# Expert gates of a decoder block: one-hot tables from key numbers in PSUM, one more transpose bank, and another order of gathered rows

## The chip, the cores and the metric

One core of one Trainium2 chip runs the whole kernel. The metric is the device time of one execution in microseconds (us); for the kernel before it is the median of three executions.

## What is computed

One decoder layer on 1024 tokens of width 1024, all in float32. The part that matters here is the second half, a product-key retrieval over 128 x 128 = 16384 single-neuron experts: each token has 8 heads, each head picks 16 experts, so a token has 128 picks, each with a first key number, a second key number and a gate.

```
idx = e1 * N_KEYS + e2
gates = jax.nn.softmax(sc, axis=-1)
u = peer_u[ix]
a = jax.nn.gelu(jnp.einsum('td,thkd->thk', hx, u), approximate=False)
vsel = peer_v[ix]
return jnp.einsum('thk,thkd->td', gx * a, vsel)
```

The first half (adaptive norm, one input projection, sliding-window attention beside a short gated convolution, an output projection) runs ahead of it for each group of tokens.

## The kernel before, in words

The tokens are eight tiles of 128. Three stages do the first half, the query projection (`lin_g0q`, `lin_g1q`, `lin_g2q`) and the choice of experts (`top16`, `pairs_head`): the groups are tiles 0 to 2, 3 to 5, and 6 and 7 (tile names with g0, g1, g2). Then follows a long last stage, `dense_experts`.

Two ways lead through the experts. Tiles 0, 1, 3, 4 and 5 are **dense**: every one of the 16384 experts is computed for them by matmul (line 1107 for u, line 1153 for v), and the gates are a table G of experts by tokens, kept in DRAM (`G_d`). Tiles 2, 6 and 7 are **sparse**: the 128 picks of each token are gathered row by row from `peer_u` and `peer_v` by indirect DMAs that GpSimd issues (line 942); VectorE multiplies each gathered u by h2 and sums it (line 963), and adds each gathered v, weighted, to an accumulator (line 970). Both h2 and the accumulator lie in PSUM.

**Dense gates** (`dense_gates1`, lines 792 to 852) make G for one dense tile. `select` (lines 660 to 718) turns ranks into key numbers, three transposes put picks on partitions and tokens on the free dimension (eT, gT), and then tokens go in groups of four, 32 groups for a tile and 160 for the five tiles. For a group, VectorE compares a table of 0 to 127 (`iota4`, bf16, in SBUF) with the second key numbers (line 808, 128 x 512, float32 out) and with the first ones (line 815, 128 x 512, bf16 out). The first table is multiplied by the gates into `og`, on GpSimd (line 825) for two groups of three and on ScalarE (line 821, four instructions) for the third. Four matmuls (line 837) make 128 x 128 of G each, into one PSUM bank; ScalarE copies it out (line 840), and each eighth group starts a DMA to `G_d` (line 845, issued by ScalarE). The matmuls of a group are written behind the tables of the next one (`pend`). There are three buffers for the line 808 table, two for the line 815 table and three for `og`.

**PSUM** has eight banks. From the second stage on, h2 takes two, the accumulator two, the projections two (`ps_a`) and everything else two (`ps_t`: transposes, attention scores, keys, G).

**Order.** The first three stages are written as generators that are run beside each other at fixed rates: in the second stage the gates of tiles 0 and 1 and the first picks of tile 2, in the third stage the gates of tiles 3, 4 and 5. The order in which each engine then takes these instructions is set by a planner with its own costs. The last stage is written out by hand (`manual_schedule`), with the remaining picks paced beside the matmuls (`Beside.run`). In it VectorE, ScalarE and GpSimd split the weights into high and low parts, weigh and add (lines 1074 to 1160). A generator `sparse_experts` (lines 902 to 981) holds the order of the picks: chunks of eight, the v rows of a chunk behind the u rows of the next one. Behind each chunk of u come one Gelu (line 928, ScalarE) and one gate multiplication (line 930, VectorE). The rows of the next tile's h2 are fetched by SyncE (line 933) and copied to PSUM by ScalarE (line 936) behind the tile's last u. Three row buffers serve the gathers in the first stages, seven in the last.

Of the kernel before, what the change touches and what calls it, by code (L numbers as in the profile page):

```python
# [9 lines left out]
F32 = mybir.dt.float32  # L10
# [5 lines left out]
ALU = mybir.AluOpType  # L16
# [68 lines left out]
def block_kernel(  # L85
# [67 lines left out]
    with ExitStack() as fctx:  # L153
# [36 lines left out]
        for i in range(7):  # L190
            pt = bank("t", f"selT_ps{i}")
            nc.tensor.transpose(pt[:14, :P], sel[:, i, :], ident)
            nc.vector.tensor_copy(selT[:, i, :], pt[:14, :P])
        iota4 = sl_.tile([P, NK, 4], BF16, name="iota4")
        nc.gpsimd.iota(
            iota4, pattern=[[1, NK], [0, 4]], base=0, channel_multiplier=0, allow_small_or_imprecise_dtypes=True
        )
        class Weights:

# [460 lines left out]
        def select(i):  # L660

            sc_ = scv[i]
            if i in SPARSE:
                gt = cst.tile([P, P], F32, tag="gates", name=f"gates{i}", bufs=len(SPARSE))
            else:
                gt = sl_.tile([P, P], F32, tag="gatesd", name=f"gates{i}")
            g3 = gt.rearrange("p (k h) -> p h k", h=8)
            nc.vector.tensor_tensor(g3, sc_, sc_[:, :, 0:1].to_broadcast([P, 8, 16]), op=ALU.subtract)
            nc.scalar.activation(gt, gt, AF.Exp)
            gsu = sl_.tile([P, 8], F32, tag="gs", name=f"gs{i}")  # L670
            nc.vector.tensor_reduce(gsu, g3, axis=mybir.AxisListType.X, op=ALU.add)
            nc.vector.reciprocal(gsu, gsu)
            gk = gt.rearrange("p (k h) -> p k h", h=8)
            nc.vector.tensor_tensor(gk, gk, gsu.unsqueeze(1).to_broadcast([P, 16, 8]), op=ALU.mult)
            gates[i] = gt
            yield 2.5

            cu = sl_.tile([P, P], U32, tag="cu", name=f"cu{i}")
            nc.vector.tensor_copy(cu.rearrange("p (k h) -> p k h", h=8), ci[i].rearrange("p h k -> p k h"))
            t0 = sl_.tile([P, P], U32, tag="t0", name=f"t0_{i}")  # L680
            nc.vector.tensor_scalar(t0, cu, 56.0, None, op0=ALU.add)
            nc.vector.tensor_scalar(t0, t0, 3, None, op0=ALU.logical_shift_right)
            fa = sl_.tile([P, P], F32, tag="fa", name=f"fa{i}")
            nc.vector.tensor_scalar(fa, t0, 8.0, 0.0, op0=ALU.subtract, op1=ALU.max)
            t1 = sl_.tile([P, P], F32, tag="t1", name=f"t1_{i}")
            nc.vector.tensor_scalar(t1, cu, 72.0, 0.0, op0=ALU.subtract, op1=ALU.max)
            ca = sl_.tile([P, P], BF16, tag="ca", name=f"ca{i}")
            nc.vector.tensor_tensor(ca, fa, t1, op=ALU.add)
            nc.vector.tensor_scalar(t0, cu, 7, None, op0=ALU.bitwise_and)
            nc.vector.scalar_tensor_tensor(fa, cu, 72.0, t0, op0=ALU.is_lt, op1=ALU.mult)  # L690
            nc.vector.tensor_scalar(t1, cu, 8.0, 8.0, op0=ALU.is_ge, op1=ALU.mult)
            nc.vector.scalar_tensor_tensor(t1, cu, 16.0, t1, op0=ALU.is_lt, op1=ALU.mult)
            cb = sl_.tile([P, P], BF16, tag="cb", name=f"cb{i}")
            nc.vector.tensor_tensor(cb, fa, t1, op=ALU.add)
            yield 2.5

            ef = []
            for s, cc in ((0, ca), (1, cb)):
                e = sl_.tile([P, P], F32, tag=f"e{s}", name=f"e{i}{s}")
                for q in range(2):  # L700
                    sl = slice(64 * q, 64 * q + 64)
                    eq = sl_.tile([P, 16, 64], BF16, tag="eq", name=f"eq{i}{s}{q}")
                    nc.vector.tensor_tensor(  # L703
                        eq.rearrange("p a (k q) -> p a k q", q=4),
                        cc[:, sl].rearrange("p (k q) -> p k q", q=4).unsqueeze(1).to_broadcast([P, 16, 16, 4]),
                        iota4[:, 0:16, :].unsqueeze(2).to_broadcast([P, 16, 16, 4]),
                        op=ALU.is_equal,
                    )
                    eq4 = eq.rearrange("p a (k h) -> p a k h", h=8)
                    nc.vector.tensor_tensor(  # L710
                        eq4, eq4, tb[i][:, s, :, :].unsqueeze(2).to_broadcast([P, 16, 8, 8]), op=ALU.mult
                    )
                    for m in (8, 4, 2):
                        nc.vector.tensor_tensor(eq[:, 0:m, :], eq[:, 0:m, :], eq[:, m : 2 * m, :], op=ALU.add)  # L714
                    nc.vector.tensor_tensor(e[:, sl], eq[:, 0, :], eq[:, 1, :], op=ALU.add)
                    yield 2.5
                ef.append(e)
            return ef
# [73 lines left out]
        def dense_gates1(gg, i):  # L792
# [10 lines left out]
            for tg in range(P // TG):  # L803
                stg = gg.tile([P, NK, TG], F32, tag="stg", name=f"stg{i}_{tg}", bufs=2)
                for q in range(TG // 4):
                    t0 = tg * TG + q * 4
                    oh2 = gg.tile([P, 4, NK], F32, tag="oh2", name=f"oh2_{i}_{t0}", bufs=3)
                    nc.vector.tensor_tensor(  # L808
                        oh2,
                        iota4.rearrange("p e t -> p t e"),  # L810
                        eT[:, 1, t0 : t0 + 4].unsqueeze(2).to_broadcast([P, 4, NK]),
                        op=ALU.is_equal,
                    )
                    oh1 = gg.tile([P, NK, 4], BF16, tag="oh1", name=f"oh1_{i}_{t0}", bufs=2)
                    nc.vector.tensor_tensor(  # L815
                        oh1, iota4, eT[:, 0, t0 : t0 + 4].unsqueeze(1).to_broadcast([P, NK, 4]), op=ALU.is_equal
                    )
                    og = gg.tile([P, 4, NK], F32, tag="og", name=f"og_{i}_{t0}", bufs=3)
                    if q % 3 == 2:
                        for k in range(4):  # L820
                            nc.scalar.activation(  # L821
                                og[:, k, :], oh1[:, :, k], AF.Copy, scale=gT[:, t0 + k : t0 + k + 1]
                            )
                    else:
                        nc.gpsimd.tensor_tensor(
                            og,
                            oh1.rearrange("p e t -> p t e"),
                            gT[:, t0 : t0 + 4].unsqueeze(2).to_broadcast([P, 4, NK]),
                            op=ALU.mult,
                        )  # L830
                    if pend:
                        pend.pop()()

                    def matmuls(oh2=oh2, og=og, stg=stg, tg=tg, q=q):
                        ps = bank("t", f"G{i}_{tg}_{q}")
                        for k in range(4):
                            nc.tensor.matmul(  # L837
                                ps[:, k * NK : (k + 1) * NK], oh2[:, k, :], og[:, k, :], start=True, stop=True
                            )
                        nc.scalar.copy(  # L840
                            stg[:, :, q * 4 : q * 4 + 4].rearrange("p e t -> p t e"),
                            ps.rearrange("p (t e) -> p t e", t=4),
                        )
                        if q == TG // 4 - 1:
                            nc.scalar.dma_start(
                                G_d.rearrange("b p g f -> p g b f")[:, tg0 + tg],
                                stg.rearrange("p (b e) t -> p b (e t)", e=GB),
                            )

                    pend.append(matmuls)  # L850
                    yield 1.2
# [50 lines left out]
        def sparse_experts():  # L902
# [4 lines left out]
            after = dict(zip(SPARSE, SPARSE[1:]))  # L907
            for i in SPARSE:
                base = len(order)
                for ch in range(nch + 1):  # L910
                    if ch < nch:
                        order += [(i, "u", ch * CH + q) for q in range(CH)]
                    if ch > 0:
# [40 lines left out]
            for n, (i, which, j) in enumerate(order):  # L954
# [9 lines left out]
                        t, t, 1.0, h2[i], op0=ALU.mult, op1=ALU.mult, accum_out=av[i][:, j : j + 1]  # L964
                    )
                elif j == 0:
                    acc[i] = ps_g.tile([P, D], F32, tag="acc", name=f"acc{i}")
                    nc.vector.tensor_scalar(acc[i], t, wv[i][:, 0:1], None, op0=ALU.mult)
                else:
                    nc.vector.scalar_tensor_tensor(  # L970
# [37 lines left out]
        ps_g = ctx.enter_context(tc.tile_pool(name="ps_g", bufs=1, space=PSUM, reuse_waits="tile"))  # L1008
        pctx = ExitStack()
        ps_a = pctx.enter_context(tc.tile_pool(name="ps_a2", bufs=2, space=PSUM, reuse_waits="tile"))  # L1010
        ps_t = pctx.enter_context(tc.tile_pool(name="ps_t2", bufs=2, space=PSUM, reuse_waits="tile"))
        gg = fctx.enter_context(tc.tile_pool(name="gg", bufs=1, reuse_waits="tile", side="right"))
        gather = Beside(sparse_experts())
        gates_of = Beside(dense_gates(gg, [0, 1]))
# [27 lines left out]


    dp = ctx.enter_context(tc.tile_pool(name="dp", bufs=1, reuse_waits="tile"))
    ps_d = ctx.enter_context(tc.tile_pool(name="ps_d", bufs=2, space=PSUM, reuse_waits="tile"))
    ps_v = ctx.enter_context(tc.tile_pool(name="ps_v", bufs=2, space=PSUM, reuse_waits="tile"))

# [335 lines left out]
```

## Time and profile before

| what | us |
|---|---|
| median of 3 executions (lowest, highest) | 2988.57 (2981.08, 2991.96) |
| the profiled execution's own time | 2981.43 |
| its span | 2979.7 |
| first stage (tiles 0 to 2) | 0 to 326 |
| second stage (tiles 3 to 5; gates of tiles 0, 1) | 326 to 728 |
| third stage (tiles 6, 7; gates of tiles 3, 4, 5) | 728 to 1137 |
| last stage (experts) | 1137 to 2980 |

The stage borders are read from the first and last instructions of each group's projections. PE is TensorE's matmuls and PEld its weight loads, DVE is VectorE, ACT is ScalarE, POOL is GpSimd, SP is SyncE. All times in the rows are microseconds from the start of the span unless they are marked ns; L808 is line 808 of the kernel before.

### The profile page before, as it was taken

What the parts mean: (1) busy time and instruction counts of PE and PEld (TensorE: products, weight loads), DVE (VectorE), ACT (ScalarE), POOL (GpSimd) and SP (SyncE); (2) the same over time, 40 slices, a digit from 0 to 9 for tenths busy, and PEclk for the clock granted to TensorE, in tenths of its full rate; (3) what the DMA queues carried; (4) which work ended last, traced back from release to release, by engine and by line L of the source; (5) the groups of instructions that cost most, each with busy time, mean ns of one, the idle gap of its engine ahead of it and who ended that gap; (6) DMA issues with size and microseconds to landing.
All of it is one profiled execution on the core that took longest, in us unless ns stands there. A gap on an engine that the chain in (4) does not pass through costs nothing.

```text
span 2979.7 us, 44185 instructions
## 1 busy us (share of the span) xinstructions
PE 2707.6 (91%) x15358; PEld 2453.9 (82%) x15358; DVE 2301.6 (77%) x4853; ACT 1102.2 (37%) x2217; POOL 1952.5 (66%) x1893
## 2 busy tenths in 40 slices
PE   5999878888687785999999999999999999999997
PEld 5789766778667775899999989999999899999996
DVE  8926997769958787777777777777787777777776
ACT  3445445574455753222222222222222222222222
POOL 3435655657536584678777767777777687777771
PEclk9999878899888997999999999999999999999999
DMA  8535247663344563898998989988998898988984
GB/s 326 187 100 170 85 134 225 185 179 105 92 108 118 164 178 118 295 329 315 329 334 318 328 295 343 337 326 312 338 332 308 314 343 325 332 323 323 330 321 150
DMA packets 381978, 750.61 MB, mean 252 GB/s; under 512 B 188598, under 2 KB 194742, under 8 KB 381756
## 3 DMA queue, kind: packets, MB, share of 16 engines
q0 software_dynamic: 110592, 402.70, 37.0%
q1 hardware_dynamic: 107004, 303.16, 29.6%
q10 hardware_dynamic: 164160, 41.94, 5.9%
q8 instruction: 120, 1.97, 0.3%
q14 instruction: 102, 0.84, 0.1%
HBM read 695.79 MB, written 51.92 MB: 251 GB/s over the span
## 4 chain that ended last, share of the span: by engine, by line
PE 60%; DVE 8%; ACT 2%; DMA 2%; POOL 1%; issue 1%; SPq 0%; DVEq 0%; ACTq 0%; POOLq 0%
PE A L1107 28%; PE V L1153 27%; DVE oh L808 1%; DVE oh L815 1%; PE G L837 1%; DVE eq L714 1%; PE lin_g2q L263 1%; DMA xr<-x1d 1%; PE lin_g2o L263 0%; DVE eq L710 0%; PE lin_g2in L263 0%; ACT stg L840 0%; ACT og L821 0%; POOL L L220 0%; DVE eq L703 0%
## 5 line engine op out<-in xcount | busy, mean ns | idle before, releaser
L220 POOL TENSOR_TENSOR L<-raw,H 128x512 fp32r<-128x512 f32 x252 | 348.0, 1392 | 286.1 <-ACT H L219 184.1
L942 POOL DMA_INDIRECT u<-in_peer_u_dram,idx x384 | 366.2, 954 | 246.0 <-DVE acc L970 96.5
L1153 PE MATMUL V<-VH,WH 128*128 128x512 f32 x1280 | 502.0, 392 | 10.3 <-DVE acc_d L1160 10.3
L942 POOL DMA_INDIRECT v<-in_peer_v_dram,idx x384 | 364.7, 950 | 216.3 <-DVE u L963 105.0
L1153 PE MATMUL V<-VH,WL 128*128 128x512 f32 x1280 | 500.7, 391 | 0.0
L1153 PE MATMUL V<-VL,WH 128*128 128x512 f32 x1280 | 499.4, 390 | 0.0
L970 DVE SCALAR_TENSOR_TENSOR acc<-v,wv,acc 128x1024 f32<-128x1024 f32 x381 | 489.0, 1283 | 12.7 <-DMA v<-in_peer_v_dram,idx 8.9
L1112 ACT ACTIVATE A<-A 128x384 f32<-128x384 f32 (+1 forms) x256 | 107.9, 422 | 988.6 <-PE A L1107 973.9
L963 DVE SCALAR_TENSOR_TENSOR u<-u,h 128x1024 f32<-128x1024 f32 x384 | 457.1, 1213 | 5.3 <-DMA u<-in_peer_u_dram,idx 5.1
L1107 PE MATMUL A<-hDH,UH 128*128 128x384 f32 (+1 forms) x2048 | 346.8, 312 | 31.8 <-DVE WL L1128 30.3
L1107 PEld LDWEIGHTS A<-hDH,UH 128*128 128x128 f32 x2048 | 323.5, 191 | 42.8 <-DVE WL L1128 31.6
L1094 POOL TENSOR_TENSOR VL<-V,VH 128x512 fp32r<-128x512 f32 x256 | 331.7, 1309 | 35.0 <-ACT VH L1090 32.7
L1107 PE MATMUL A<-hDH,UL 128*128 128x384 f32 (+1 forms) x2048 | 342.2, 309 | 10.4 <-POOL UL L1078 10.4
L1107 PE MATMUL A<-hDL,UH 128*128 128x384 f32 (+1 forms) x2048 | 342.5, 309 | 0.0
L1078 POOL TENSOR_TENSOR UL<-U,UH 128x1024 fp32r<-128x1024 f32 x128 | 309.2, 2416 | 36.4 <-ACT UH L1074 34.2
L1124 DVE TENSOR_TENSOR A<-A,Gb 128x384 f32<-128x384 f32 (+1 forms) x256 | 126.5, 497 | 261.2 <-ACT A L1112 257.3
L1107 PEld LDWEIGHTS A<-hDH,UL 128*128 128x128 f32 x2048 | 310.5, 189 | 11.4 <-POOL UL L1078 11.4
L1107 PEld LDWEIGHTS A<-hDL,UH 128*128 128x128 f32 x2048 | 312.6, 190 | 0.0
L1153 PEld LDWEIGHTS V<-VH,WH 128*128 128x128 f32 x1280 | 241.0, 188 | 57.8 <-DVE acc_d L1160 12.4
L1153 PEld LDWEIGHTS V<-VH,WL 128*128 128x128 f32 x1280 | 241.2, 188 | 52.4
L837 PE MATMUL G<-og,oh 128*128 128x128 f32 x1280 | 207.9, 322 | 80.2 <-ACT stg L840 29.0
L1153 PEld LDWEIGHTS V<-VL,WH 128*128 128x128 f32 x1280 | 241.3, 189 | 46.3
(310 smaller groups left out, 4567.3 us busy)
## 6 DMA issues: line engine op xcount, KB each, us to landing
U<-in_peer_uT_dram SPq DMA_DIRECT2D x128, 512.0 KB, 7.9
V<-in_peer_v_dram SPq DMA_DIRECT2D x256, 256.0 KB, 4.0
G_d<-stg ACTq DMA_DIRECT2D x20, 2048.0 KB, 13.8
Gb<-G_d SPq DMA_DIRECT2D x64, 640.0 KB, 7.7
raw<-in_w_in_dram SPq DMA_DIRECT2D x54, 512.0 KB, 3.6
wada<-in_w_ada_dram SPq DMA_DIRECT2D x48, 512.0 KB, 5.5
raw<-in_w_query_dram SPq DMA_DIRECT2D x48, 512.0 KB, 3.6
raw<-in_w_out_dram SPq DMA_DIRECT2D x24, 512.0 KB, 3.8
```

The costliest lines, as they stand in the source:

```text
L220: nc.gpsimd.tensor_tensor(L, src, H.bitcast(F32), op=ALU.subtract)
L263: nc.tensor.matmul(ps[:, :w], wt[:, c, :], h[:, q * (NC // 2) + c, o : o + w], start=(k == 0), stop=(k == 3 * NC - 1),)
L837: nc.tensor.matmul(ps[:, k * NK : (k + 1) * NK], oh2[:, k, :], og[:, k, :], start=True, stop=True)
L942: nc.gpsimd.indirect_dma_start(out=t, out_offset=None, in_=peer_u if which == "u" else peer_v, in_offset=bass.IndirectOffsetOnAxis(ap=idx[ ...
L963: nc.vector.scalar_tensor_tensor(t, t, 1.0, h2[i], op0=ALU.mult, op1=ALU.mult, accum_out=av[i][:, j : j + 1])
L970: nc.vector.scalar_tensor_tensor(acc[i], t, wv[i][:, j : j + 1], acc[i], op0=ALU.mult, op1=ALU.add)
L1078: nc.gpsimd.tensor_tensor(L, Ur.pop(b), Up[b][0].bitcast(F32), op=ALU.subtract)
L1094: nc.gpsimd.tensor_tensor(L, Vr.pop(v), Vp[v][0].bitcast(F32), op=ALU.subtract)
L1107: nc.tensor.matmul(ps[:, : n * P], u[:, c, :], h[:, c, sl], start=(k == 0), stop=(k == 3 * NC - 1))
L1112: nc.scalar.activation(w, w, AF.Gelu)
L1124: nc.vector.tensor_tensor(w3, w3, g, op=ALU.mult)
L1153: nc.tensor.matmul(ps, w[:, ts_], v, start=(n == 0), stop=(n == 3 * CB - 1))
```

## The change

A table of 0 to 127 in float32 is made by GpSimd and copied by ScalarE into a PSUM bank of its own (`keyno`) when the second stage begins. One VectorE instruction compares it with both key numbers of a group and writes both one-hot tables into one float32 buffer of 128 x 1024, of which there are three. The gate multiplication, on the same engines as before, overwrites the first table in place. `iota4` shrinks to 16 numbers, which is what `select` needs. The accumulator of the sparse tiles is no longer allocated with h2 but in a pool of the last stage, and the two banks become the third `ps_t` bank and the bank of `keyno`. For tile 2 all 128 u rows are now ahead of its 128 v rows; tiles 6 and 7 keep the chunked order.

```diff
-        iota4 = sl_.tile([P, NK, 4], BF16, name="iota4")
+        iota4 = sl_.tile([P, 16, 4], BF16, name="iota4")
         nc.gpsimd.iota(
-            iota4, pattern=[[1, NK], [0, 4]], base=0, channel_multiplier=0, allow_small_or_imprecise_dtypes=True
+            iota4, pattern=[[1, 16], [0, 4]], base=0, channel_multiplier=0, allow_small_or_imprecise_dtypes=True
+        )
+        iota = fs.tile([P, NK], F32, name="iota")
+        nc.gpsimd.iota(
+            iota, pattern=[[1, NK]], base=0, channel_multiplier=0, allow_small_or_imprecise_dtypes=True
         )
...
-                        iota4[:, 0:16, :].unsqueeze(2).to_broadcast([P, 16, 16, 4]),
+                        iota4.unsqueeze(2).to_broadcast([P, 16, 16, 4]),
...
-                    oh2 = gg.tile([P, 4, NK], F32, tag="oh2", name=f"oh2_{i}_{t0}", bufs=3)
+
+                    oh = gg.tile([P, 2, 4, NK], F32, tag="oh", name=f"oh_{i}_{t0}", bufs=3)
                     nc.vector.tensor_tensor(
-                        oh2,
-                        iota4.rearrange("p e t -> p t e"),
-                        eT[:, 1, t0 : t0 + 4].unsqueeze(2).to_broadcast([P, 4, NK]),
+                        oh,
+                        keyno.unsqueeze(1).unsqueeze(1).to_broadcast([P, 2, 4, NK]),
+                        eT[:, :, t0 : t0 + 4].unsqueeze(3).to_broadcast([P, 2, 4, NK]),
                         op=ALU.is_equal,
                     )
-                    oh1 = gg.tile([P, NK, 4], BF16, tag="oh1", name=f"oh1_{i}_{t0}", bufs=2)
-                    nc.vector.tensor_tensor(
-                        oh1, iota4, eT[:, 0, t0 : t0 + 4].unsqueeze(1).to_broadcast([P, NK, 4]), op=ALU.is_equal
-                    )
-                    og = gg.tile([P, 4, NK], F32, tag="og", name=f"og_{i}_{t0}", bufs=3)
+                    og, oh2 = oh[:, 0], oh[:, 1]
                     if q % 3 == 2:
                         for k in range(4):
                             nc.scalar.activation(
-                                og[:, k, :], oh1[:, :, k], AF.Copy, scale=gT[:, t0 + k : t0 + k + 1]
+                                og[:, k, :], og[:, k, :], AF.Copy, scale=gT[:, t0 + k : t0 + k + 1]
                             )
                     else:
                         nc.gpsimd.tensor_tensor(
-                            og,
-                            oh1.rearrange("p e t -> p t e"),
-                            gT[:, t0 : t0 + 4].unsqueeze(2).to_broadcast([P, 4, NK]),
-                            op=ALU.mult,
+                            og, og, gT[:, t0 : t0 + 4].unsqueeze(2).to_broadcast([P, 4, NK]), op=ALU.mult
                         )
...
-                for ch in range(nch + 1):
+                if i == SPARSE[0]:
+
+                    order += [(i, "u", j) for j in range(P)] + [(i, "v", j) for j in range(P)]
+                for ch in range(nch + 1 if i != SPARSE[0] else 0):
...
-                    acc[i] = ps_g.tile([P, D], F32, tag="acc", name=f"acc{i}")
+                    acc[i] = ps_c.tile([P, D], F32, tag="acc", name=f"acc{i}")
...
-        ps_t = pctx.enter_context(tc.tile_pool(name="ps_t2", bufs=2, space=PSUM, reuse_waits="tile"))
+        ps_t = pctx.enter_context(tc.tile_pool(name="ps_t2", bufs=3, space=PSUM, reuse_waits="tile"))
+        ps_i = pctx.enter_context(tc.tile_pool(name="ps_i", bufs=1, space=PSUM))
+        keyno = ps_i.tile([P, 512], F32, name="keyno")[:, :NK]
+        nc.scalar.copy(keyno, iota)
...
+    ps_c = ctx.enter_context(tc.tile_pool(name="ps_c", bufs=1, space=PSUM, reuse_waits="tile"))
```

## Rows read from the trace of the kernel before

**Rows 1.** The page: busy time of each engine over the whole span.
```profile
PE 2707.6 (91%) x15358; PEld 2453.9 (82%) x15358; DVE 2301.6 (77%) x4853; ACT 1102.2 (37%) x2217; POOL 1952.5 (66%) x1893
```
**Rows 2.** Stretches: length, busy time (count) per engine, granted clock, DMA share, GB/s.
```profile
372.00:640.00 268.00, 215.88 (x1157) 182.80 (x1156) 218.22 (x391) 153.74 (x322) 156.49 (x125) 0.85 0.62 183
640.00:728.00 88.00, 85.76 (x537) 84.78 (x535) 74.02 (x488) 47.72 (x90) 58.93 (x129) 0.99 0.47 136
728.00:1137.00 409.00, 307.80 (x2037) 277.82 (x2037) 335.52 (x927) 228.38 (x449) 239.92 (x267) 0.87 0.47 133
...
1215.00:2980.00 1765.00, 1734.74 (x9707) 1578.34 (x9705) 1346.56 (x1993) 482.28 (x947) 1293.15 (x1093) 0.99 0.88 318
```
**Rows 3.** Chain of waits from 793 to 1083 us: share of that stretch by line.
```profile
by line: DVE oh L808 14.1%; DVE oh L815 13.5%; PE G L837 12.8%; PE lin_g2o L263 4.6%; PE lin_g2in L263 4.6%; ACT stg L840 4.2%; DVE eq L714 4.1%; issue 3.8%; ACT og L821 3.7%; PE lin_g2q L263 3.5%; PE S L357 2.6%; ACT Ss L387 2.6%; PE po L4
```
**Rows 4.** Lines 808 and 815 by themselves: shortest, median and longest ns.
```profile
L808 DVE TENSOR_TENSOR oh<-iota,eT x160: 668/684/2259, 372.3 to 1096.0; 128x512 f32<-128x512 bf16 x160
...
L815 DVE TENSOR_TENSOR oh<-iota,eT x160: 374/418/1742, 372.9 to 1080.0; 128x512 bf16<-128x512 bf16 x160
```
**Rows 5.** Groups by line: busy us, mean ns of one, idle before and releasers.
```profile
L808 DVE TENSOR_TENSOR oh<-iota,eT 128x512 f32<-128x512 bf16 x160 | 147.8, 931 | 39.3 <-PE G L837 38.0 <-ACT eT L799 1.1
L815 DVE TENSOR_TENSOR oh<-iota,eT 128x512 bf16<-128x512 bf16 x160 | 115.9, 734 | 12.5 <-POOL og L825 6.8 <-ACT og L821 5.4
```
**Rows 6.** VectorE with PSUM operands (L963, L522) and without (L530): shortest, median, longest ns.
```profile
L963 DVE SCALAR_TENSOR_TENSOR u<-u,h x384: 1161/1214/1223, 422.6 to 2885.8; 128x1024 f32<-128x1024 f32 x192
...
L522 DVE SCALAR_TENSOR_TENSOR zg<-lin_g1in,vec,ccg x4: 606/614/617, 381.0 to 529.6; 128x384 f32<-128x384 f32 x4
...
L530 DVE SCALAR_TENSOR_TENSOR cvg<-zg,vec,cvg x24: 469/612/1825, 92.2 to 930.4; 128x384 f32<-128x384 f32 x16, 128x256 f32<-128x256 f32 x8
```
**Rows 7.** VectorE's additions with a PSUM operand (L1160), all runs of the line.
```profile
L1160 DVE TENSOR_TENSOR acc_d<-acc_d,V x310: 670/683/690, 1265.7 to 2968.2; 128x512 f32<-128x512 f32 x155
```
**Rows 8.** Line 808 by stretch: length, VectorE busy time (count), granted clock, DMA.
```profile
372.00:450.00 78.00, 16.67 (x20) 0.78 0.46 129
...
728.00:1137.00 409.00, 89.66 (x96) 0.87 0.47 133
```
**Rows 9.** Line 815 by stretch, the same columns.
```profile
372.00:450.00 78.00, 13.76 (x22) 0.78 0.46 129
...
728.00:1137.00 409.00, 70.35 (x96) 0.87 0.47 133
```
**Rows 10.** All engines from 372 to 450 us, columns as in rows 2.
```profile
372.00:450.00 78.00, 61.96 (x295) 50.84 (x294) 73.70 (x160) 37.05 (x73) 41.80 (x33) 0.78 0.46 129
```
**Rows 11.** What TensorE waited for, 372 to 1137 us: total us, times, longest.
```profile
PE G L837 <- ACT stg L840: 29.0, 17, 5.0
PE G L837 <- POOL og L825: 17.2, 12, 5.4
PE G L837 <- DVE oh L808: 12.4, 10, 4.0
```
**Rows 12.** What GpSimd waited for, 372 to 1100 us, the same columns.
```profile
POOL L L220 <- ACT H L219: 92.7, 35, 13.2
POOL og L825 <- DVE oh L815: 52.1, 46, 4.0
POOL og L825 <- PE G L837: 49.1, 25, 8.2
```
**Rows 13.** GpSimd gate product and float32 subtraction: shortest, median, longest ns.
```profile
L825 POOL TENSOR_TENSOR og<-oh,gT x120: 1038/1336/4117, 373.5 to 1097.9; 128x512 f32<-128x512 bf16 x120
...
L220 POOL TENSOR_TENSOR L<-raw,H x252: 1258/1297/2251, 20.7 to 1122.3; 128x512 fp32r<-128x512 f32 x126
```
**Rows 14.** Line 928 (Gelu) in the second stage.
```profile
L928 ACT ACTIVATE wv<-av x3: 208/208/209, 460.4 to 551.6; 128x8 f32<-128x8 f32 x3
L928 ACT ACT_TABLE_LOAD  x2: 1283/1283/1283, 459.1 to 550.2; - x2
```
**Rows 15.** Chain of waits where the last stage begins: start us, us, what.
```profile
1134.65 2.35 POOL UL L1078
1137.05 5.94 PE A L1107 x32
```
**Rows 16.** Last copies out of the `ps_t` banks (line 625).
```profile
L625 ACT COPY Skg<-pkg x48: 356/478/484, 256.5 to 1126.6; 128x384 f32<-128x384 f32 x32, 128x256 f32<-128x256 f32 x16
```

## Prediction, made before the changed kernel was run

> **What bounds the kernel now.** I read the page's first part, then the table by stretches, because a share over the whole span mixes stages. TensorE is busy 91% of the span [rows 1], but unevenly [rows 2]: in the last stage it is busy for 1735 of 1765 us and nothing that the change touches is late there; at the end of the second stage (640 to 728) for 86 of 88. In the two stretches in which gates are made it is not: 216 of 268 us (372 to 640) and 308 of 409 us (728 to 1137), so 52 + 101 = 153 us are open there, at a granted clock of 0.85 and 0.87 where the filled stretch has 0.99. VectorE is busy 218 of 268 and 336 of 409 us, 82% in both. Then the chain of waits: from 793 to 1083 us it runs through lines 808 and 815 for 14.1% and 13.5% of 290 us [rows 3], 80.0 us, more than through any other line. So what the change can win lies in about 680 us in front of the last stage, and there first in VectorE's two comparisons.
>
> Why these are long is seen in one line each. Their medians are 684 and 418 ns, but single ones take 2259 and 1742 [rows 4], and the means are 931 and 734 [rows 5]: a pair takes 1.665 us where 1.102 would do. VectorE instructions with a PSUM operand show nothing of this: 606 to 617 ns in the same second stage, 1161 to 1223 for 1024 elements in any stage, whereas a like one with both tensors in SBUF goes from 612 to 1825 [rows 6]. The long ones are those that overlap GpSimd's work on SBUF.
>
> **Part 1, one instruction from PSUM.** It removes two instructions of 128 x 512 and adds one of 128 x 1024 with one PSUM and one SBUF input. The price: an addition of 512 with a PSUM operand takes 683 ns [rows 7], a product of 1024 with one 1214 ns [rows 6]; I take 1.214 us, with the shortest, 1.161, and twice 0.683 = 1.366 as ends. The uncontended pair was cheaper by 0.112; the pair as it ran was dearer by 1.665 - 1.214 = 0.451 us. On the chain that counts 80.0 / 1.665 = 48 times: **-21.7 us** in the third stage. Below it is nothing, if the chain goes on elsewhere; above it is all 96 groups of that stage, 89.66 + 70.35 us [rows 8, 9] against 96 x 1.214 = 116.5, so -43.5. In the second stage VectorE is full only from 372 to 450, 73.7 of 78 us [rows 10]; there 21 pairs took 16.67 + 13.76 = 30.43 us [rows 8, 9] and will take 25.49: **-4.9 us**. Later in that stage I count nothing, since the gathered rows, the projection and the attention lie beside it; the end above is all 64 pairs at 0.451, -28.9.
>
> By the Trainium skill (VectorE: DVE Perf Modes, The perf-mode tier table) a tensor_tensor with all operands of 16 bits in SBUF runs at twice the rate, and any PSUM operand brings it back to the plain one. That speaks against the change, and the trace agrees where nothing overlaps: 418 against 684 ns [rows 4]. By that rule alone 160 groups would cost 160 x 0.112 = 17.9 us more of VectorE. Against it stands another (SBUF — State Buffer, Who interferes with whom): a VectorE instruction with two SBUF inputs and a GpSimd one that reads SBUF shut each other out for a whole instruction, one with a single SBUF input does not. [Rows 6] agree with that too, and in this stage, with GpSimd at work for 59% of it, the second outweighs the first.
>
> **Part 2, the product in place.** GpSimd's product of bf16 numbers takes 1336 ns in the median, its float32 subtraction of the same size 1297 [rows 13], so 120 products change by about -5 us, between 120 x (1258 - 1336) = -9 and nothing, on an engine that is busy for 240 of 409 us: 0 on the path. It also no longer waits itself while a VectorE comparison holds it up (the longest took 4117 ns); I count nothing for that. The same count of ScalarE elements: 0.
>
> But the loop gets longer. Before, the bf16 table of the next group could be made while all three `og` were in use, and GpSimd then waited for TensorE and began at once: 49.1 us in 25 waits [rows 12]. Now the whole table stands in the buffer that TensorE holds; at a release VectorE first writes for 1.214 us, and behind it on VectorE wait top-16, attention and `select`. Nothing in the trace shows it directly. At the least it is 0; if each of the 25 waits costs one comparison, 30.4 us; if each of 160 / 3 = 53 rounds of three buffers does, 64.3. I take half of the 25, because the next part makes releases come sooner: **+15.2 us**.
>
> **Part 3, the third bank.** TensorE waits 29.0 us in 17 waits for ScalarE to copy G out of one of two banks [rows 11]. A third one lets a group of matmuls start one copy earlier. Between nothing and all 29.0 I take half, since a ScalarE that is late for several groups is late with three banks too: **-14.5 us**. Late next would be the 17.2 us for GpSimd's product and the high and low weights, for which GpSimd waits 92.7 us [rows 12].
>
> **Part 4, the order of tile 2.** The second stage now takes as many rows as before, all of them u. Line 963 costs 1.214 and line 970 nearly the same, so VectorE keeps its sum; GpSimd issues as many DMAs, from the same queue and with three buffers. One more chunk is full, so at most one more Gelu with its table load, 0.21 + 1.28 us of ScalarE [rows 14], beside an engine that is busy for 154 of 268 us: 0. In the last stage tile 6's h2 is fetched by SyncE 120 rows earlier, one DMA among hundreds, and copied when tile 2's last u is done: 0. VectorE, GpSimd and SyncE have the same list there.
>
> **Part 5, small moves.** Two smaller number tables instead of one, before anything waits for GpSimd; one ScalarE copy at the start of the second stage; 0. The last stage's first matmuls now lie in banks that `ps_t` held. The last copy out of these starts at 1126.6 [rows 16], and the first matmul waits for GpSimd's low part until 1137.05 [rows 15]: 10 us of cover, so 0; without the cover it would be one copy, 0.4 us.
>
> **The sum.** -21.7 - 4.9 - 14.5 + 15.2 = -25.9 us, against the profiled execution's own 2981.4: 2955.5. That execution was among the fastest; the median of three is 7.1 higher. I put half of this on top: **2959 us**.
>
> **The rivals.** *The clock follows.* If the open 153 us close by half, TensorE is steadier, and the granted clock, now a mixture of its two levels (1.2 and 2.4 GHz) at a mean of 0.86, may go halfway to the 0.99 of the filled stretch, to 0.925. The 524 us of matmuls in the two stretches would shrink by up to 1 - 0.86 / 0.925 = 7%, 37 us more: 2922. For it speaks that the second stage reaches 0.99 as soon as TensorE has no gaps [rows 2]; against it that the projections still wait for weights.
>
> *The gain is hidden.* The planner's order has other waits close behind: GpSimd for ScalarE's high part, 92.7 us [rows 12], and TensorE for tables of either engine. If these end last, or the PSUM operand does not spare the wait as [rows 6] suggest, VectorE's shorter time turns into idle time: 2985, between 2974 and 2996. Against it, the chain goes through VectorE's comparisons and not through the weights where the gates are made [rows 3].
>
> *Slower: the buffer loop binds.* The mechanism is in part 2: one VectorE comparison more between TensorE's release and the next product. If every round of three is bound by it, 64.3 us come on top of -21.7 - 4.9 - 14.5: +23.2, so 3008 with the same 3.5 as above. It decides once more than 41.1 / 1.214 = 34 of the 53 rounds wait; before, 25 of GpSimd's products did.
>
> **How the numbers follow.** The forecast has a chance of 0.51, with 2930 to 2973 as its own range; the clock 0.14; the hidden gain 0.19; the buffer loop 0.16. Half a per cent, 15 us, is what a measurement of this kernel can tell from no change; the forecast and the clock lie below that, so faster is 0.65, same 0.19, slower 0.16. The range must reach down to the clock's 2922 and up to most of the slower case: 2920 to 3005 leaves out about a tenth at either side.
>
> **What would show it.** One VectorE instruction a group at 1.2 us with hardly any spread; the two lines' 263.7 us become about 194. TensorE's wait for the copy of G falls to half; VectorE's wait for TensorE's release (38.0 us, 30 times [rows 5]) grows if the loop matters. The third stage should give most, some 15 to 20 us, the last stage nothing. It is wrong if the comparison takes over 1.4 us or spreads, if the last stage changes by over 5 us, or if the third stage keeps its 409 us with VectorE less busy.

## The result, and the profile after

The changed kernel takes 2910.08 us in the median (2906.1 to 2911.93), against 2987.48 for the kernel before in the same comparison: a ratio of 0.9743, with a 95% interval from 0.9725 to 0.9761. It is faster by 77 us, where the prediction had counted on 26; 2910 lies below its range. In what follows, runs are compared by their ratios to the kernel before on the same chip; 0.001 of a ratio is 3.0 us.

The page of the changed kernel, busy time over a span of 2909.9 us (against [rows 1]):

```profile
PE 2675.3 (92%) x15358; PEld 2432.7 (84%) x15358; DVE 2236.2 (77%) x4693; ACT 1099.3 (38%) x2219; POOL 1905.2 (65%) x1894
```

VectorE has 160 instructions fewer, one for each group, and 65 us less work; GpSimd, whose list of products is the same, has 47 us less. TensorE's 15358 matmuls are the same and were busy for 32 us less.

Its table by stretches, cut at the changed kernel's own borders (columns as in [rows 2], where the stretches were 268, 88, 409 and 1765 us):

```profile
372.00:621.00 249.00, 206.38 (x1162) 177.81 (x1160) 194.74 (x342) 155.51 (x323) 139.74 (x125) 0.87 0.69 197
621.00:710.00 89.00, 86.52 (x542) 85.78 (x540) 76.60 (x502) 48.35 (x93) 60.31 (x135) 0.99 0.47 137
710.00:1068.00 358.00, 290.42 (x2047) 265.16 (x2048) 289.05 (x820) 223.49 (x449) 214.07 (x262) 0.90 0.58 153
...
1145.00:2910.00 1765.00, 1732.09 (x9698) 1576.71 (x9696) 1351.28 (x1974) 482.59 (x946) 1291.90 (x1092) 0.99 0.88 318
```

The two stretches with gates became 19 and 51 us shorter; the filled stretch and the last stage are as they were. The granted clock in them went from 0.85 and 0.87 to 0.87 and 0.90.

The comparison and the gate product by themselves (shortest, median, longest ns; against [rows 4] and [rows 13]):

```profile
L813 DVE TENSOR_TENSOR oh<-keyno,eT x160: 1182/1214/1227, 373.5 to 1025.0; 128x1024 f32<-128x1024 f32 x160
...
L826 POOL TENSOR_TENSOR oh<-oh,gT x120: 1029/1040/2022, 375.1 to 1027.7; 128x512 f32<-128x512 f32 x120
```

The comparison costs what the prediction took, 1.214 us, without spread. What the prediction did not count is in the second line: the product's median fell from 1336 to 1040 ns, which is about the shortest of before (1038), and its longest from 4117 to 2022. In all the 120 products took 156.7 us before and take 131.5.

The chain of waits from 765 to 1030 us of the changed kernel, by line (against [rows 3]):

```profile
by line: PE G L835 12.8%; DVE oh L813 10.1%; issue 9.0%; ACT stg L838 8.8%; POOL L L224 6.3%; PE lin_g2in L267 6.0%; ACT oh L822 4.6%; PE lin_g2o L267 4.6%; POOL oh L826 4.5%; DMA raw<-in_w_query_dram 2.9%; PE po L419 2.6%; PE lin_g2q L267 
```

VectorE's tables went from 27.6% of that stretch to 10.1%. No line stands out any more: the chain changes between TensorE, VectorE, ScalarE and GpSimd, whose product (4.5%) and weights (`L`, 6.3%) are now among its first lines.

What TensorE waited for between 360 and 1068 us (total us, times, longest; against [rows 11]):

```profile
PE G L835 <- POOL oh L826: 38.4, 26, 4.8
```

The wait for the copy of G, 29.0 us before, is not among the longest any more (2.4 us in 5 waits are left of it); the wait for the product, 17.2 before, is now the first. VectorE's wait for TensorE's release, 38.0 us before [rows 5], in the 30 waits that the prediction names, is now longer:

```profile
DVE oh L813 <- PE G L835: 51.5, 40, 7.0
```

### The profile page after: what moved, and what is told of

Its sections match the earlier page's. It is cut to its first block, busy times and chain, and to the rows that moved or that the text cites. A ratio compares the mean times of both kernels' runs of the same rounds, so it can differ in the third digit from the quotient of the medians.

```text
span 2909.9 us, 44039 instructions
## 1 busy us (share of the span) xinstructions
PE 2675.3 (92%) x15358; PEld 2432.7 (84%) x15358; DVE 2236.2 (77%) x4693; ACT 1099.3 (38%) x2219; POOL 1905.2 (65%) x1894
## 4 chain that ended last, share of the span: by engine, by line
PE 61%; DVE 5%; ACT 2%; POOL 2%; DMA 2%; issue 1%; SPq 0%; ACTq 0%; DVEq 0%; POOLq 0%
PE A L1112 30%; PE V L1158 28%; PE G L835 1%; DVE oh L813 1%; ACT stg L838 1%; DMA xr<-x1d 1%; POOL L L224 1%; PE lin_g2in L267 1%; DVE eq L718 0%; ACT oh L822 0%; PE lin_g2o L267 0%; POOL oh L826 0%; DMA raw<-in_w_query_dram 0%; DMA Gb<-G_d 0%; DVE eq L707 0%
## 5 line engine op out<-in xcount | busy, mean ns | idle before, releaser
L224 POOL TENSOR_TENSOR L<-raw,H 128x512 fp32r<-128x512 f32 x252 | 335.3, 1341 | 290.0 <-ACT H L223 202.1
L1165 DVE TENSOR_TENSOR acc_d<-acc_d,V 128x512 f32<-128x512 f32 x310 | 211.6, 683 | 88.6 <-PE V L1158 88.5
```

Of the source, the lines that this page charges most:

```text
L224: nc.gpsimd.tensor_tensor(L, src, H.bitcast(F32), op=ALU.subtract)
L1165: nc.vector.tensor_tensor(accs[0][:, t, hs], accs[0][:, t, hs], ps, op=ALU.add)
```

## The experiments

All ran on the chip beside the kernel before. Two pairs of reasons had to be told apart: which part gave how much, and through which engine.

**Tables and bank apart.** The changed kernel with two banks:

```diff
-        ps_t = pctx.enter_context(tc.tile_pool(name="ps_t2", bufs=3, space=PSUM, reuse_waits="tile"))
+        ps_t = pctx.enter_context(tc.tile_pool(name="ps_t2", bufs=2, space=PSUM, reuse_waits="tile"))
```

> The changed kernel with two ps_t banks instead of three (the key numbers stay in a PSUM bank, one bank lies idle). Theory A (most of the 77 us comes from the comparison that GpSimd no longer holds up, on VectorE and on GpSimd): 2915 to 2940, and GpSimd's product stays at 1.04 us in the median. Theory B (most comes from the third bank): 2955 to 2985, with TensorE waiting for the copy of G for 25 us or more.

Measured: 2934.83 us, ratio 0.9837 (0.9801 to 0.9873). TensorE's waits in it, 360 to 1137 us, show the two-bank wait again at its old size:

```profile
PE G L835 <- ACT stg L838: 31.4, 30, 5.1
```

The other way round, the old tables with three banks (the two comparisons and three kinds of buffers as in the code before; the accumulator in the last stage's pool, tile 2's u rows first):

```diff
-                    oh = gg.tile([P, 2, 4, NK], F32, tag="oh", name=f"oh_{i}_{t0}", bufs=3)
...
+                    oh2 = gg.tile([P, 4, NK], F32, tag="oh2", name=f"oh2_{i}_{t0}", bufs=3)
...
+                    oh1 = gg.tile([P, NK, 4], BF16, tag="oh1", name=f"oh1_{i}_{t0}", bufs=2)
...
+                    og = gg.tile([P, 4, NK], F32, tag="og", name=f"og_{i}_{t0}", bufs=3)
```

> The kernel before with the accumulator moved, tile 2's u rows first and three ps_t banks, but the two old comparisons and separate buffers. Theory A: 2960 to 2985, since the bank alone gives at most the 29 us that TensorE waited for the copy of G. Theory B: 2915 to 2945.

Measured: 2961.75 us, ratio 0.9923 (0.99 to 0.9945). And the same with two banks, so that only the order of tile 2 and the accumulator's place differ from the kernel before:

> The kernel before with the accumulator moved and tile 2's u rows first, with two banks and the old tables. Both theories: no change that can be measured, 2975 to 2995. Theory C (the planner's other order alone makes the difference): 2960 or less.

Measured: 2989.33 us, ratio 1.0012 (0.9993 to 1.003): no change that can be measured, so part 4 of the change is worth nothing here. Beside it the other three make a square:

| ratio | two banks | three banks | the bank |
|---|---|---|---|
| old tables | 1.0012 | 0.9923 | -27 us |
| new tables | 0.9837 | 0.9743 | -28 us |
| the tables | -52 us | -54 us | |

By the intervals of the ratios each difference is uncertain by some 10 us. Within that the two parts add, and neither is seen to depend on the other. Theory B, that the bank gives most, falls; so does a pure effect of the order that came with part 4. The planner's order of the other three runs differs as well, and what that alone does in them was not tested.

**Where the tables' gain comes from.** One operand changed; in the two traces every engine has the same instructions in the same order:

```diff
-                        keyno.unsqueeze(1).unsqueeze(1).to_broadcast([P, 2, 4, NK]),
+                        iota.unsqueeze(1).unsqueeze(1).to_broadcast([P, 2, 4, NK]),
```

> The changed kernel with the comparison reading the key numbers from SBUF instead of PSUM; every engine has the same instructions in the same order. Theory A: the comparison's mean rises from 1.21 to 1.6 us or more, GpSimd's product to 1.2 us or more, and the time goes back to between 2935 and 2965. Theory B or C: within 8 us of the changed kernel's 2910, since banks and order are the same.

Measured: 2975.58 us, ratio 0.9975 (0.9964 to 0.9986): 0.0232 or 69 us above the changed kernel, more than the range that was expected. The groups by line of this run (busy us, mean ns, idle before) show both engines slowed by the one operand:

```profile
L224 POOL TENSOR_TENSOR L<-raw,H 128x512 fp32r<-128x512 f32 x252 | 366.7, 1466 | 265.6 <-ACT H L223 166.8 <-PE lin_g0in L267 53.4 <-PE lin_g0o L267 16.8
...
L813 DVE TENSOR_TENSOR oh<-iota,eT 128x1024 f32<-128x1024 f32 x160 | 249.8, 1583 | 54.2 <-PE G L835 41.5 <-POOL L L224 7.4 <-POOL oh L826 3.1
...
L826 POOL TENSOR_TENSOR oh<-oh,gT 128x512 f32<-128x512 f32 x120 | 176.6, 1480 | 112.4 <-DVE oh L813 104.7 <-DVE nm L383 4.2 <-PE lin_g1in L267 3.4
```

The same groups of the changed kernel:

```profile
L224 POOL TENSOR_TENSOR L<-raw,H 128x512 fp32r<-128x512 f32 x252 | 335.3, 1341 | 290.0 <-ACT H L223 202.1 <-PE lin_g0in L267 37.7 <-PE lin_g0o L267 18.6
...
L813 DVE TENSOR_TENSOR oh<-keyno,eT 128x1024 f32<-128x1024 f32 x160 | 190.7, 1214 | 57.8 <-PE G L835 51.5 <-POOL L L224 3.9 <-ACT eT L803 1.9
...
L826 POOL TENSOR_TENSOR oh<-oh,gT 128x512 f32<-128x512 f32 x120 | 131.5, 1100 | 110.9 <-DVE oh L813 100.5 <-DVE nm L383 4.2 <-PE lin_g1in L267 3.8
```

VectorE loses 59 us and GpSimd 45 in the product and 31 in the weights. GpSimd's share is on the path: in the chain of waits from 780 to 1085 us of this run the product and the weights have 25.0% of 305 us, 76 us, against 10.8% of 265 us, 29 us, in the changed kernel; VectorE's comparison went from 27 to 43 us.

```profile
by line: DVE oh L813 14.2%; POOL oh L826 12.7%; POOL L L224 12.3%; issue 10.6%; PE G L835 8.5%; PE lin_g2in L267 4.8%; ACT stg L838 4.5%; PE po L419 2.3%; DVE eq L718 2.3%; ACT oh L822 2.2%; PE hbg L459 2.0%; PE lin_g2q L267 1.6%; DVE eq L7
```

With the keys in SBUF the new form is a loss: it is 0.0052, 16 us, slower than the old tables with three banks. The whole gain of the tables, and more, is the PSUM operand. The 16 us are not the price of the form alone, though: against the old tables with three banks VectorE's tables are 18 us shorter in this run (249.8 against 156.5 + 111.8), while GpSimd's product is 23 us longer (176.6 against 154.0) and its weights 24 (366.7 against 343.1), so they too hold time in which GpSimd was held up.

**Which engine's half is on the path.** Each half was put back by itself, as nearly as it goes. For GpSimd, a product with one behind each gate product:

```diff
...
+                        nc.gpsimd.tensor_tensor(
+                            og[:, 0, 0:112], og[:, 0, 0:112], one, op=ALU.mult
+                        )
```

> The changed kernel with one more GpSimd product behind each of the 120 gate products, 112 numbers of og times one, about 0.38 us: as much as the gate product lost when the key numbers were read from SBUF (1.100 to 1.480 us in the mean), 46 us of GpSimd in all, with the comparison left at 1.21 us. Theory A1 (GpSimd's half of the lock-out is on the path): 25 to 45 us above the changed kernel, 2935 to 2955. Theory A2 (only VectorE's half is on the path, as the prediction counted): within 10 us of 2910.

Measured: 2942.77 us, ratio 0.9847 (0.9822 to 0.9871): 0.0104, 31 us above the changed kernel. The addition took 423 ns in the median and 456 in the mean, 54 us in all:

```profile
L831 POOL TENSOR_TENSOR oh<-oh,one x120: 412/423/1283, 379.1 to 1070.6; 128x112 f32<-128x112 f32 x120
```

The longest, 1283 ns, is three times the median: the addition can be held up itself, and it holds VectorE up too. VectorE's work rose by 14 us, 11 of them in the copies of two numbers at L524 and L529, whose medians went from 162 and 164 ns to 665 and 616. So not all of the 31 us need be GpSimd's own.

For VectorE, a part of each comparison again, from PSUM, which nothing holds up here:

```diff
+                    nc.vector.tensor_tensor(
+                        oh[:, 0, 0:2, 0:102],
+                        keyno[:, 0:102].unsqueeze(1).to_broadcast([P, 2, 102]),
+                        eT[:, 0, t0 : t0 + 2].unsqueeze(2).to_broadcast([P, 2, 102]),
+                        op=ALU.is_equal,
+                    )
```

> The changed kernel with one more VectorE comparison from PSUM behind each of the 160, over 204 numbers it has already written, about 0.37 us: as much as the comparison lost when the key numbers were read from SBUF (1.214 to 1.583 us in the mean), 59 us of VectorE in all, and nothing that GpSimd can hold up. Theory A1: within 15 us of 2910. Theory A2: 40 us or more above it, 2950 or more. A split of the 65 us over both engines: about 25 us above in this run and in the run with longer GpSimd products.

Measured: 2938.06 us, ratio 0.9834 (0.9816 to 0.9852): 27 us above. The addition took 365 ns, 58 us in all, and GpSimd's products did not become longer:

```profile
L819 DVE TENSOR_TENSOR oh<-keyno,eT x160: 308/365/373, 377.0 to 1058.0; 128x204 f32<-128x204 f32 x160
```

Neither A1 nor A2 holds alone; the split that the second expectation named does. With both additions:

> The changed kernel with both additions at once: 0.42 us of GpSimd behind each of its 120 products and 0.37 us of VectorE behind each of the 160 comparisons. If the two halves of the lock-out lie one behind the other on the path, they add: 33 + 28 = 61 us above the changed kernel, 2965 to 2980, which is also where the key numbers in SBUF came out (2976). If they cover each other: 2940 to 2955.

Measured: 2977.51 us, ratio 0.997 (0.9959 to 0.9981): 0.0227, 68 us above the changed kernel. In total the two add (31 + 27 = 58, and some more), and the run comes out where the keys in SBUF did. By stage they do not add, so that the total agrees is partly luck. At the first matmul of `lin_g1q`, where the second stage's stretch with gates ends, the profiled executions with GpSimd longer, VectorE longer and both longer are 20, 15 and 23 us behind the changed kernel, and the one with the keys in SBUF 18; from the first matmul of `lin_g2in` to the first of the experts they take 17, 15 and 39 us more, and the one with the keys in SBUF 46. TensorE's waits for the product in this run and in the run with the keys in SBUF, 360 to 1137 us, are alike:

```profile
PE G L846 <- POOL oh L837: 67.4, 42, 5.5
```

```profile
PE G L835 <- POOL oh L826: 70.4, 41, 7.1
```

TensorE waits for the product for 38.4 us in the changed kernel and some 70 when both engines are slow. In the run with GpSimd longer alone it is 72.7, so this wait does not tell the two halves apart. In these additions the planner's order is not the same as in the changed kernel, so a few us of either can be order; and the weights, 31 us longer with the keys in SBUF, were not put back.

**The buffer loop.** Four buffers instead of three. To make room, the number table is made in a buffer of the keys, and two temporaries of `select` share their buffers with the key numbers:

```diff
-                    oh = gg.tile([P, 2, 4, NK], F32, tag="oh", name=f"oh_{i}_{t0}", bufs=3)
+                    oh = gg.tile([P, 2, 4, NK], F32, tag="oh", name=f"oh_{i}_{t0}", bufs=4)
...
-                e = sl_.tile([P, P], F32, tag=f"e{s}", name=f"e{i}{s}")
+                e = sl_.tile([P, P], F32, tag=("fa", "t1")[s], name=f"e{i}{s}")
```

> The changed kernel with four buffers for the two tables instead of three (the number table made in another buffer, and two tags of select shared, to make room). If the longer buffer loop costs the 15 us that the prediction put down for it: 2885 to 2900, and VectorE's wait for TensorE's matmuls of G (51.5 us in 40 waits) falls to half. If the loop is not bound by its buffers: 2905 to 2915.

Measured: 2895.18 us, ratio 0.9697 (0.9677 to 0.9717), 14 us below the changed kernel and the best form found up to here. VectorE's wait fell, not to half:

```profile
DVE oh L809 <- PE G L831: 36.7, 28, 7.8
```

And TensorE's two waits for the product and the copy, 360 to 1137 us:

```profile
PE G L831 <- POOL oh L822: 15.2, 14, 1.6
...
PE G L831 <- ACT stg L834: 10.3, 8, 4.3
```

So three buffers bind the loop of the changed kernel, for about what the prediction put down. That the change made the loop longer is a different thing. A part of it, that one instruction writes both tables, was tested by two instructions into buffers of their own (three each, from PSUM, the product in place):

```diff
+                    oh2 = gg.tile([P, 4, NK], F32, tag="oh2", name=f"oh2_{i}_{t0}", bufs=3)
...
+                    og = gg.tile([P, 4, NK], F32, tag="og", name=f"og_{i}_{t0}", bufs=3)
```

> The changed kernel with the two tables written by two instructions of 128 x 512 from PSUM into buffers of their own, three each, the product still in place. Two take 2 x 0.683 = 1.366 us against 1.214, 24 us of VectorE in all. If the merging matters only by that time: 2910 to 2930. If it costs the loop (both tables wait for the same buffer): below 2908.

Measured: 2919.88 us, ratio 0.9774 (0.9756 to 0.9793), 9 us above the changed kernel. Two take 2 x 0.681 us instead of 1.214, 24 us of VectorE in all, and by the rate of the longer comparisons (27 us for 58) that alone is 11, an estimate. So one instruction instead of two costs the loop nothing that can be seen. It does not test what the prediction meant: here too the product is in place, and the first table stands in a buffer that TensorE holds, where the kernel before had buffers apart for it. Old tables with one more buffer, or new ones with a buffer apart for the product, were not run.

**Sharing the products otherwise.** In both kernels ScalarE takes two groups of eight (`q % 3 == 2` with q from 0 to 7), 40 in all, and GpSimd 120; it is not one group of three. On top of four buffers, ScalarE takes three groups of eight (`q in (1, 4, 6)`) or one (`q == 4`) instead of two:

> The kernel with four buffers, and ScalarE takes the gate product of three groups of eight instead of two. GpSimd loses 20 products of 1.04 us, ScalarE gains 80 instructions of 0.39. If GpSimd's time is still what ends last: 2880 to 2892. If ScalarE is by now as late as GpSimd: 2893 to 2910.

Measured: 2911.61 us, ratio 0.975 (0.9734 to 0.9766), just above the second range.

> The kernel with four buffers, and ScalarE takes one group of eight. GpSimd gains 20 products of 1.04 us. If GpSimd's time ends last, by the rate of the longer products (33 us for 51 us more): 2905 to 2912. If ScalarE's four instructions for a group (1.55 us) are the longer way: 2885 to 2894.

Measured: 2893.24 us, ratio 0.9689 (0.9665 to 0.9712). More for ScalarE costs 16 us; less is not told from four buffers alone, since the intervals overlap. The first of the two readings for it, that GpSimd's time ends last, falls: with four buffers 20 more products on GpSimd, and 20 fewer on ScalarE, together cost nothing that can be seen. So what GpSimd's time costs depends on the buffers: with three, 54 us more of it cost 31. Four buffers are faster than both kernels (14 us below the changed one, uncertain by some 8).

## Why the prediction was right and wrong

**Right in kind.** The place (the two stretches with gates, nothing in the last stage), the price of the comparison (1.214 us), the cause of the long ones, the order of tile 2 at nothing and GpSimd's product as the next late thing all came as written. By the Trainium skill (SBUF — State Buffer, Who interferes with whom) a VectorE instruction with two SBUF inputs and a GpSimd one that reads SBUF block each other, in either direction; the run with the keys in SBUF shows both directions, 1.583 against 1.214 us on VectorE and 1.480 against 1.100 on GpSimd. The prediction's "one with a single SBUF input does not" is too wide: VectorE's copies of two numbers (L525) took from 111 to 1249 ns before, and their median rose when GpSimd was made longer.

**The step that failed** is in part 2: "It also no longer waits itself while a VectorE comparison holds it up (the longest took 4117 ns); I count nothing for that", and with it "0 on the path" for the product. The lock-out (each engine waiting for the other's reads of SBUF) was costed on VectorE's side alone. The product's price was read from a median, 1336 ns, which already held the hold-ups; its shortest, 1038 in the same row [rows 13], is what it takes in the changed kernel. And it was put at nothing on the path because GpSimd was busy for only 240 of 409 us; the chain of waits before lists no GpSimd line among its first either [rows 3]. The runs showed in its place: the PSUM operand is worth 69 us against the same form with the keys in SBUF, on both engines together; 54 us more of GpSimd behind the products cost 31, about as much as 58 more of VectorE (27); and with the keys in SBUF GpSimd's two lines have 25.0% of the chain. An engine with 40% idle time is not off the path if another often waits for it: TensorE waited for the product 12 times before [rows 11], 26 times in the changed kernel and 41 times with the keys in SBUF, for 120 products.

**VectorE's own term** was put at -21.7 - 4.9 = -26.6. Its tables took 263.7 us before and take 190.7; by the rate of the longer comparisons (27 us for 58) the 73 us are worth 34, an estimate. By the rate of the longer products (31 us for 54) the 25 us by which GpSimd's gate products fell against the kernel before are worth 14 more, and 34 + 14 is near the 52 to 54 that the tables gave. So VectorE's sum was near, but its place was not: longer comparisons cost 15 us in either stage, and the second stage gave 19 us and the third 51, where the prediction had some 15 to 20 in the third and less in the second.

**The third bank** was put at half of its upper bound, -14.5; it gave 27 to 28, near the bound itself. With the new tables ScalarE was not late with three banks: TensorE's wait for its copies is 31.4 us with two and 2.4 with three. With the old tables that wait fell only from 26.0 to 11.4 us while the time fell by 27, and VectorE's wait for TensorE fell from 40.9 to 15.1; so there the agreement with the row of 29.0 is partly luck.

**The longer loop**, +15.2, stays open. With three banks and the old tables VectorE waited for TensorE's release for 15.1 us and GpSimd for 38.5; in the changed kernel VectorE waits for 51.5 and GpSimd not at all. So the wait moved from GpSimd to VectorE, which fits part 2, but in sum it did not grow. The 14 us that a fourth buffer gives show that three bind; whether they bind more than before was not tested.

So the account is: tables -53 where -26.6 + 15.2 = -11.4 stood; bank -27 where -14.5 stood; order 0.

One reading in part 5 was wrong without harm: the first matmul of the last stage does not wait until 1137.05 but starts at 1127.95, so the cover behind the copy of 1126.6 [rows 16] was some 1 us and not 10.

**The rivals.** The buffer loop did not decide, though VectorE's waits for TensorE rose from 30 to 40, beyond the 34 at which the prediction let it decide: a whole comparison for each further wait, as it was priced, is not what the runs bear out. The gain was not hidden. The clock did follow in part: the granted clock is 0.02 and 0.03 higher in the two stretches, and TensorE's busy time is 32 us lower for the same matmuls. How much of the 77 us would be there without it was not separated.

## What to carry to other kernels

A constant that VectorE reads beside an SBUF operand can lie in PSUM; where GpSimd works at the same time, that can free both engines, and here it more than repaid the slower float32 form. Count a lock-out on both of its sides, take the price of an instruction from its shortest runs and not from a median that holds the hold-ups, and ask for each side how often another engine waits for it, not how busy it is. Where a wait for a buffer or a bank has its own row, do not halve it without a reason: here, in one case, the whole row was nearer.

## What the runs showed of the hardware

VectorE and GpSimd held each other up where both read SBUF, and not where VectorE's second operand lay in PSUM. In the trace of the changed kernel 107 of the 160 comparisons lie beside a GpSimd instruction that is no DMA issue, and none takes over 1227 ns. With the keys in SBUF 75 of them take over 15% more than the shortest, the longest 2330 ns, and each of the 75 lies beside such an instruction.

A GpSimd instruction can be held through several VectorE instructions: with the keys in SBUF the longest product took 4557 ns, against 1032 for the shortest. The line of that run, and two lines of its timeline (start us, us):

```profile
L826 POOL TENSOR_TENSOR oh<-oh,gT x120: 1032/1155/4557, 373.2 to 1090.2; 128x512 f32<-128x512 f32 x120
...
384.30 4.56 POOL L826 TENSOR_TENSOR oh<-oh,gT 128x512 f32<-128x512 f32 x1 [4.37 <-DVE oh L813]
...
385.28 2.35 DVE L813 TENSOR_TENSOR oh<-iota,eT 128x1024 f32<-128x1024 f32 x2
```

During that product VectorE ran five instructions without a gap, from 384.15 to 387.96 us, all with two tensors in SBUF, the two comparisons among them; the product ended at 388.86. That it got in only behind the last of them is read from this one case.
